# SiLU-gated split on one core: 16 rows per partition, two loads and one store of a shared output buffer

## The chip, the core and the metric

The kernel runs on one core of a Trainium2 chip. The core has five instruction streams, of which this kernel uses four: ACT (ScalarE), which applies functions elementwise, DVE (VectorE), which multiplies, SP (SyncE), which only issues transfers here, and a few constants written by POOL (GpSimd). Data move between the device's memory (HBM) and the on-chip buffers (128 partitions, each with its own stretch of memory) by DMA: an engine issues a transfer on its own queue, and 16 DMA engines, shared by all queues, carry it out. The metric is device time in microseconds (us), the median of the runs; lower is better. The profile is of one execution.

## The reference

```python
def setup_inputs():
    batch, seq, dim = (32, 512, 2048)
    return {'x': np.random.randn(batch, seq, dim).astype(np.float32)}

def reference(x: np.ndarray) -> np.ndarray:
    half_dim = x.shape[-1] // 2
    x1, x2 = (x[..., :half_dim].copy(), x[..., half_dim:].copy())
    silu_x1 = x1 * (1 / (1 + np.exp(-x1)))
    return (silu_x1 * x2).astype(np.float32)
```

There are 32 x 512 = 16,384 rows of 2,048 float32 values. SiLU of a row's first half is multiplied with its second half. The input has 134.2 MB, the output 67.1 MB, and each byte is moved once.

## The kernel before

The rows are cut into 16 tiles of 1,024 rows. In a tile, each of the 128 partitions takes K = 8 consecutive rows: 64 KiB of input in one piece of HBM, and 32 KiB of output in one piece. Neighbouring partitions of a tile lie 64 KiB apart in the input and 32 KiB apart in the output, so a tile is one closed stretch of 8 MiB in and 4 MiB out.

There are two input buffers (`in_pool`, bufs=2, L35) of 64 KiB per partition and two output buffers (`out_pool`, bufs=2, L36) of 32 KiB per partition. The function `load(i)` (L43 to L46) takes an input buffer and issues the transfer of tile i from SP (L45). Loads 0 and 1 are issued ahead of the loop; load i+2 is issued at the end of step i (L71). It goes into the buffer that tile i used, and so it waits on SP until the last multiply of tile i has read it.

A step of the loop (L50) handles one tile in four chunks of KC = 2 rows per partition. For each chunk, ACT writes SiLU of the first half into the output buffer `ot` (L56), and DVE multiplies it there with the second half (L61). After the fourth chunk ACT issues the store of the tile (L69). This instruction stands in ACT's stream behind the tile's activations and waits for the last multiply, and what follows on ACT waits with it. In the last tile each chunk is stored by itself, also from ACT (L67), 1 MiB at a time.

The order of everything else is set by buffers. The framework adds the waits: an activation waits for the load of its tile, and, where it is the first to write an output buffer again, for the landing of the store that last read that buffer. With two output buffers this is the store of two tiles earlier. Loads travel on SP's ring and stores on ACT's ring; within a ring transfers go in the order of their issue.

Of the kernel before, what the change touches and what calls it, by code (L numbers as in the profile page):

```python
# [1 line left out]

# [4 lines left out]


@with_exitstack
def kernel(  # L10
    ctx: ExitStack,
    tc: tile.TileContext,
    x: bass.AP,
    out: bass.AP,
):

    nc = tc.nc
    P = nc.NUM_PARTITIONS

    x_flat = x.flatten_outer_dims()
    out_flat = out.flatten_outer_dims()
    num_rows, in_cols = x_flat.shape
    half = in_cols // 2
    dt = x_flat.dtype

    K = 8  # L30
    KC = 2
    n_tiles = num_rows // (P * K)
    assert n_tiles * P * K == num_rows

    in_pool = ctx.enter_context(tc.tile_pool(name="in_pool", bufs=2))  # L35
    out_pool = ctx.enter_context(tc.tile_pool(name="out_pool", bufs=2))  # L36

    xv = x_flat.rearrange("(n p k) d -> n p k d", p=P, k=K)
    ov = out_flat.rearrange("(n p k) d -> n p k d", p=P, k=K)

    loaded = {}

    def load(i):  # L43
        xt = in_pool.tile([P, K, in_cols], dt, name="xt")
        nc.sync.dma_start(out=xt, in_=xv[i])  # L45
        loaded[i] = xt  # L46

    load(0)
    load(1)
    for i in range(n_tiles):  # L50
        xt = loaded.pop(i)
        last = i == n_tiles - 1
        ot = out_pool.tile([P, K, half], dt, name="ot")
        for c in range(0, K, KC):
            ce = c + KC
            nc.scalar.activation(  # L56
                out=ot[:, c:ce, :],
                in_=xt[:, c:ce, :half],
                func=mybir.ActivationFunctionType.Silu,
            )  # L60
            nc.vector.tensor_mul(  # L61
                out=ot[:, c:ce, :],
                in0=ot[:, c:ce, :],
                in1=xt[:, c:ce, half:],
            )
            if last:
                nc.scalar.dma_start(out=ov[i][:, c:ce, :], in_=ot[:, c:ce, :])  # L67
        if not last:
            nc.scalar.dma_start(out=ov[i], in_=ot)  # L69
        if i + 2 < n_tiles:  # L70
            load(i + 2)  # L71


# [1 line left out]
_INS = ['x']  # L75
_OUTS = [((32, 512, 1024), 'float32')]


# [23 lines left out]
```

## Time and profile before

| what | value |
|---|---|
| median of 3 runs | 471.87 us (471.72 to 472.5) |
| the profiled execution | 471.92 us |
| its span, first to last instruction | 470.1 us |
| DVE busy, 64 multiplies of 2,286 ns in the mean | 142.4 us, 30% |
| ACT busy, 64 activations of 1,898 ns in the mean | 118.3 us, 25% |
| bytes moved | 201.35 MB, 428 GB/s over the span |
| load, issue to landing (median of 16) | 47.1 us |
| store of a tile, issue to landing (median of 15) | 39.7 us |
| store of a chunk in the last tile (median of 4) | 5.4 us |

In the lines quoted from the profile an operation stands as line, engine, name, output <- input with partitions x elements, and count. L56 is line 56 of the kernel. In the timeline a line begins with its start and its length in us, and the bracket at its end tells how long the engine had been idle and what ended that. SPq and ACTq are the queues on which SP and ACT issue transfers; q1 is the DMA ring of SP's transfers and q10 that of ACT's. For a ring, the numbers are packets, MB moved, and the time its packets took as a share of the time of all 16 DMA engines. The row of digits after "DMA" shows the busy share of the DMA engines in 40 equal slices of the span, in tenths. In the list of waits, a line names who waited, for whom, the total in us, the number of times and the longest.

### The profile page before, as it was taken

Reading aid. Unit: us, or ns where it says so; the run is one execution under the profiler, and the core shown is the slowest. Engines: PE = TensorE matmul, PEld = TensorE weight load, DVE = VectorE, ACT = ScalarE, POOL = GpSimd, SP = SyncE. Lnnn points to the kernel's source line nnn. Section 1 sums busy time; section 2 is a strip of 40 time slices with the busy share of each in tenths; the row PEclk is TensorE's granted clock in tenths of the full one; section 3 lists DMA queues with packets and bytes.
Section 4 is the critical chain, followed back from the end, with each engine's and each line's share of the span. In section 5 each row is a group of like instructions: output and inputs, shape, how many; then the busy total and the mean of one; then the engine's idle time right before and its main releaser. Section 6 shows DMA issues by size and latency. Waiting matters only on the chain.

```text
span 470.1 us, 267 instructions
## 1 busy us (share of the span) xinstructions
DVE 142.4 (30%) x64; ACT 118.3 (25%) x65; POOL 0.2 (0%) x4
## 2 busy tenths in 40 slices
DVE  0070704207052070511606115070250702407033
ACT  1050506014060240602306032060320604106041
POOL 0000000000000000000000000000000000000000
DMA  8999999999999999999999999999999999999998
GB/s 357 446 446 401 401 485 435 418 401 443 449 446 401 441 457 396 446 474 390 468 404 438 457 441 407 427 420 449 446 410 432 480 401 418 440 474 424 399 424 337
DMA packets 5042, 201.35 MB, mean 428 GB/s; under 512 B 560, under 2 KB 560, under 8 KB 560
## 3 DMA queue, kind: packets, MB, share of 16 engines
q1 hardware_dynamic: 2304, 134.22, 66.2%
q10 hardware_dynamic: 2736, 67.11, 33.1%
q14 instruction: 2, 0.02, 0.0%
HBM read 134.22 MB, written 67.11 MB: 428 GB/s over the span
## 4 chain that ended last, share of the span: by engine, by line
DMA 80%; DVE 15%; ACT 4%; issue 0%; ACTq 0%; SPq 0%
DMA xt<-in_x_dram 80%; DVE ot L61 15%; ACT ot L56 4%; SPq L45 0%; ACTq L67 0%; ACTq L56 0%
## 5 line engine op out<-in xcount | busy, mean ns | idle before, releaser
L61 DVE TENSOR_TENSOR ot<-ot,xt 128x2048 f32<-128x2048 f32 x64 | 142.4, 2286 | 322.9 <-ACT ot L56 322.9
L56 ACT ACTIVATE ot<-xt 128x2048 f32<-128x2048 f32 x64 | 117.1, 1898 | 344.0 <-DMA xt<-in_x_dram 340.4
L56 ACT ACT_TABLE_LOAD x1 | 1.3, 1283 | 0.7 <-PEq L86 0.7
L86 POOL MEMSET const-bfloat16-1.0<- 128x1 bf16 x1 | 0.1, 101 | 0.0
L86 POOL MEMSET const-uint8-127<- 128x1 uint8 x1 | 0.1, 101 | 0.0
L86 POOL MEMSET const-float32-0.0<- 128x1 f32 x1 | 0.1, 98 | 0.2 <-issue 0.2
L86 POOL MEMSET const-float32-1.0<- 128x1 f32 x1 | 0.1, 98 | 0.0
## 6 DMA issues: line engine op xcount, KB each, us to landing
out_dram<-ot ACTq DMA_DIRECT2D x15, 4096.0 KB, 39.7
out_dram<-ot ACTq DMA_DIRECT2D x4, 1024.0 KB, 5.4
xt<-in_x_dram SPq DMA_DIRECT2D x16, 47.1
```

The costliest lines, as they stand in the source:

```text
L56: nc.scalar.activation(out=ot[:, c:ce, :], in_=xt[:, c:ce, :half], func=mybir.ActivationFunctionType.Silu,)
L61: nc.vector.tensor_mul(out=ot[:, c:ce, :], in0=ot[:, c:ce, :], in1=xt[:, c:ce, half:],)
L86: nc = _bacc.Bacc("TRN2", target_bir_lowering=False, num_devices=1)
```

## The change

A partition now takes 16 consecutive rows, in two halves of 8. Tiles are numbered as before, but tiles 2m and 2m+1 are the first and the second half of the same 128 stretches: load i brings 64 KiB per partition, with neighbouring partitions 128 KiB apart in HBM. The two tiles of a pair write into one output buffer of 64 KiB per partition, of which there is one (bufs=1), and one store of 8 MiB, 64 KiB in one piece per partition, carries the pair out; it is issued from ACT after the odd tile. The last pair differs: after tile 14 ACT stores its half of the buffer (4 MiB), and the four chunks of tile 15 are stored one by one from SP. Loads, chunks, activations and multiplies keep their sizes and numbers.

```diff
-    out_pool = ctx.enter_context(tc.tile_pool(name="out_pool", bufs=2))
+    out_pool = ctx.enter_context(tc.tile_pool(name="out_pool", bufs=1))
 
-    xv = x_flat.rearrange("(n p k) d -> n p k d", p=P, k=K)
-    ov = out_flat.rearrange("(n p k) d -> n p k d", p=P, k=K)
+    xv = x_flat.rearrange("(n p h k) d -> n h p k d", p=P, h=2, k=K)
+    ov = out_flat.rearrange("(n p k) d -> n p k d", p=P, k=2 * K)
...
-        nc.sync.dma_start(out=xt, in_=xv[i])
+        nc.sync.dma_start(out=xt, in_=xv[i // 2, i % 2])
         loaded[i] = xt
...
+    ot = None
     for i in range(n_tiles):
         xt = loaded.pop(i)
-        last = i == n_tiles - 1
-        ot = out_pool.tile([P, K, half], dt, name="ot")
+        if i % 2 == 0:
+            ot = out_pool.tile([P, 2 * K, half], dt, name="ot")
+        o0 = (i % 2) * K
         for c in range(0, K, KC):
-            ce = c + KC
+            o = slice(o0 + c, o0 + c + KC)
             nc.scalar.activation(
-                out=ot[:, c:ce, :],
-                in_=xt[:, c:ce, :half],
+                out=ot[:, o, :],
+                in_=xt[:, c:c + KC, :half],
                 func=mybir.ActivationFunctionType.Silu,
             )
             nc.vector.tensor_mul(
-                out=ot[:, c:ce, :],
-                in0=ot[:, c:ce, :],
-                in1=xt[:, c:ce, half:],
+                out=ot[:, o, :],
+                in0=ot[:, o, :],
+                in1=xt[:, c:c + KC, half:],
             )
-            if last:
-                nc.scalar.dma_start(out=ov[i][:, c:ce, :], in_=ot[:, c:ce, :])
-        if not last:
-            nc.scalar.dma_start(out=ov[i], in_=ot)
+            if i == n_tiles - 1:
+                nc.sync.dma_start(out=ov[i // 2][:, o, :], in_=ot[:, o, :])
+        if i == n_tiles - 2:
+            nc.scalar.dma_start(out=ov[i // 2][:, :K, :], in_=ot[:, :K, :])
+        elif i % 2 == 1 and i < n_tiles - 2:
+            nc.scalar.dma_start(out=ov[i // 2], in_=ot)
```

## The prediction

> **What bounds the kernel now.** I read the page's DMA parts first, then the timeline of the first tiles, the waits of SP's queue, the times from issue to landing of single DMAs, and last the end of the span.
>
> ```profile
> DMA  8999999999999999999999999999999999999998
> ...
> q1 hardware_dynamic: 2304, 134.22, 66.2%
> q10 hardware_dynamic: 2736, 67.11, 33.1%
> ```
>
> q1 is the ring of SP's loads, q10 that of ACT's stores. Together their packets fill 99.3% of 16 engines' span: nothing but data movement bounds this kernel. The packet records in the trace give the unit: a 64 KiB load packet takes 2,418 ns (median of 2,048), a 32 KiB store packet 1,213 ns (1,920), an 8 KiB store packet 309 ns (512). Per engine: 128 x 2.418 + 120 x 1.213 + 32 x 0.309 = 465.0 us of the 470.1.
>
> ```profile
> 22.75 7.31 ACT L56 ACTIVATE ot<-xt 128x2048 f32<-128x2048 f32 x4 [20.74 <-DMA xt<-in_x_dram]
> 24.69 8.90 DVE L61 TENSOR_TENSOR ot<-ot,xt 128x2048 f32<-128x2048 f32 x4 [24.69 <-ACT ot L56]
> 33.62 0.38 ACTq L69 DMA_DIRECT2D out_dram<-ot  x1
> 45.89 7.31 ACT L56 ACTIVATE ot<-xt 128x2048 f32<-128x2048 f32 x4 [15.84 <-DMA xt<-in_x_dram]
> ```
>
> A tile computes in 10.85 us: 1.95 us to the first multiply, then 8.90. It hides entirely under transfers. Note where the store is issued, 33.62, and where the next tile lands, 45.89.
>
> ```profile
> SPq L45 <- DMA xt<-in_x_dram: 246.1, 14, 21.1
> SPq L45 <- DVE ot L61: 152.5, 14, 10.9
> ```
>
> A load waits for its buffer, released by the multiplies two tiles earlier. It costs nothing now, because another load and a store are always queued. Whether that stays so is the question.
>
> ```profile
> DMA to landing us min/median/max: 33.7/33.7/33.7
> ```
>
> ```profile
> DMA to landing us min/median/max: 39.7/39.7/39.7
> ```
>
> The first is the store issued at 33.62, the second that of 114.76. In its packet records the first store's opening packet starts 5.9 us after the issue, behind the load packet in progress and one more, which here took 3.37 us, 0.95 over the usual. Then each engine alternates strictly: a store packet, a load packet, and so on; 39.55 + 8 x 1.213 + 6 x 2.418 = 63.76 (recorded: the eighth ends at 63.72). Six and not seven loads, since one turn of the load ring goes to the completion packet of a finished load. The store's own completion waits one more load packet (2.42) and 1.2 us of engine skew and signal: 67.3, the landing shown. Turns go by packet, not by byte, so a 32 KiB store gets a third of an engine. That is just its demand, and the later stores (39.7) queue behind their predecessor: both rings are never empty.
>
> **What the Trainium skill says.** "DMA: Bandwidth & Descriptors", section Queues, rings and completion order: each engine goes round its queue rows at packet granularity. The trace agrees (here a packet is one whole run of a partition). The same page, Issuing engines are not separate DMA queues: DMAs of all issuers run on the same 16 engines and interleave. The trace agrees: q1 and q10 share out one time. Its section Latency and other measured facts lists losses by row pitch in HBM: 512 KiB gives 207 GB/s where full is 214, 3% off. The new pitch of 128 KiB is not listed and no run here shows it; I keep 3% as an upper bound.
>
> **The change part by part.** *Bytes and packets.* Load packets stay at 64 KiB; their partitions now lie 128 KiB apart. Store packets become 64 KiB; by 32 to 64 KiB of load I price one at 2.418 us, so 7 pair stores, one half store and 4 last pieces give 128 x 2.418 + 56 x 2.418 + 8 x 1.213 + 32 x 0.309 = 464.5 us per engine against 465.0. Gain 0.5 us at most. ACT's, DVE's and the load issues' counts don't change; 8 store issues of 0.36 us on ACT go and 4 move to SP, all in idle time. The output buffers take the same space, one of 64 KiB for two of 32.
>
> *The added wait.* With one shared buffer, the first ACTIVATE of an even tile must wait until the whole previous pair store has landed. Behind it queue that tile's other ACTIVATEs, the odd tile's, and the next store; DVE waits for ACT; and SP's next load waits for the multiplies. So for the time store landing + 10.85 no new load can start. Only two loads are in flight to cover it.
>
> *One pair*, from C, where its store and a load B are issued. Load A, issued at the even tile's end, has run three of its 8 packet rounds and is in the fourth. First store packet at C+4.9 (current and one more load packet; 5.9 in the trace, 4.9 by the steady phase). Then 8 stores and 6 loads alternate, 14 x 2.418 = 33.85; the completion waits 2.42 + 1.2: landing at C+42.4. Load B, with a half share, has 4 of 8 rounds left and ends at C+50.9, landing C+52.1. The even tile computes from C+42.4 to C+53.25; only then is the next A issued. It starts at about 1.05 us later (the very first load: 0.73 to 1.73) and its first packet takes 0.63 longer (3.05, the mean of the first 16). The engines stand idle from C+50.9 to C+54.3. The odd tile starts with B's landing and ends at C+62.95. By then A has run three rounds again, so the cycle closes: 63.0 us a pair against 24 x 2.418 = 58.03 of work. The 5.0 lost are 3.4 idle, 0.63 and 0.95 (the stretched packet at each store's start).
>
> *Start.* Tile 0 ends at 33.6 as before. Without a store beside it load 1 ends at 41.1 and lands at 42.1 (was 45.87); tile 1 ends at C0 = 52.95. The store arrives at about 54.0 in load 2's sixth round (53.1 to 55.6), lets one more, stretched to 3.37, go by, starts at 58.9 and lands at 96.4; load 3 ends already at 100.0, but load 4 can't be issued before 107.2. Idle until 108.3. C1 = 96.4 + 1.95 + 17.8 (two tiles of multiplies back to back) = 116.15. The second pair has load 4 late and comes to C2 = 180.1; then 62.9 and 63.0 each: C6 = 432.0.
>
> *End.* Store 6 lands at 474.4, tile 14 ends at 485.25 and the half store starts at 486.3, while the loads have run out at 482.9. ACT issues it ahead of tile 15's ACTIVATEs, which so start at 485.65; the last piece is computed by 496.5. From 486.3 the half store and the pieces keep the engines busy for 8 x 1.213 + 32 x 0.309 = 19.6: 505.9, with skew 506.3. The trace has 1.26 from the last packet's end to the span's: 507.6. That the pieces come from SP costs nothing: its queue has no load left.
>
> Check by the engines: 464.5 work, 2.4 start, 1.3 end, and stalls of 9.9 (first pair), about 5 x 5.0, 0.95 for store 6 and 3.4 before the half store: 507.5. The profiled execution took 471.92 for a span of 470.1, and the median of the runs is 471.87, so 1.8 is added: **509.4 us**, 37.5 slower, 8%.
>
> **The rivals.**
>
> *Store first (not slower).* If the pair store ran nearly at full rate, it would land at about C+2+19.3+1.2 = C+22.5, and the next load, issued at C+33.4, would queue long before B ended. The point from which this decides: landing + 10.85 + 1.05 before B's end at C+50.9, a landing by C+39. Time then 464.5 + 2.4 + 1.3 = 468.2, or 470.0 us with 1.8: 0.4% faster. For it: my margin is only 3.4 us a pair. Against: the trace shows strict turns, and landing inside C+39 alone leaves the 0.95 stalls (7 x 0.95) and most of the first pair's gap, so it would still be slower. Chance 5%.
>
> *One turn later.* The store's arrival falls 0.45 us ahead of a packet boundary in my steady phase. Beyond it, each store starts 2.42 later; then the even tile ends at C+55.7 and the pair at C+65.4. Six pairs make 522 of the span, 524 us. For it: the first store in the trace came 5.9 after its issue, not 4.9. Against: the phase readjusts from pair to pair. 14%.
>
> *Smaller store packets.* If a 64 KiB run of a store were cut into two of 32 KiB, a pair store would get a third of the engine until the loads run out: 11 load rounds and 16 stores, landing near C+52; pair 52 + 19.75 = 71.5, end near 568 us. For it: no 64 KiB store packet is in the trace. Against: 64 KiB load packets are. 4%.
>
> *A wider stride costs.* 3% on 309.5 us of load packets, about 9 us more: 518. 4%.
>
> *Stalls smaller.* If the 0.95 stretch and part of the issue lag come once and not for each store, the pair takes 62 and the end is near 501. 5%.
>
> **How the numbers follow.** The likeliest case, with 68%, spans 503 to 516, its phase unknown by a part of a packet. Range 500 to 525: it takes in the later turn, the stride and the smaller stalls; outside are the first and third rivals. Slower by over 0.2% (which is what a measurement of this kernel can tell) in all but the store-first rival: 95%; of its 5%, 3 faster and 2 within, as its 0.4% gain hangs on a tail without gaps.
>
> **What would show it.** Right: ACT's waits at even tiles end with the store, not the load (some 7 of them); the store lands 42 to 44 us after issue; the DMA digits fall below 9 about every 63 us, and the mean is some 396 GB/s (428 x 470.1 / 507.6); stores and loads take 2.4 us a packet alike; C0 near 53. Wrong: store landings under 39 us, or no dip between loads, would leave the time as it was; landings above 50 would mean small packets; load packets above 2.42 us in mean, the stride.

## The result, and the profile after

The changed kernel takes 511.66 us (median of 4 runs, 510.6 to 513.12) against 471.92 us (median of 4, 471.72 to 472.5): a ratio of 1.0842, with a 95% interval of 1.0809 to 1.0875. It is slower by 8.4%. The profiled execution took 510.83 us with a span of 509.1.

First the page of the changed kernel, its row of DMA digits, its DMA parts and its list of DMA issues (the last number of an issue line is the median time from issue to landing).

```profile
DMA  9999999749999799998999989999699996999968
...
DMA packets 4035, 201.34 MB, mean 396 GB/s; under 512 B 449, under 2 KB 449, under 8 KB 449
...
q1 hardware_dynamic: 2880, 138.41, 65.3%
q10 hardware_dynamic: 1152, 62.92, 28.5%
...
xt<-in_x_dram SPq DMA_DIRECT2D x16, 37.3
out_dram<-ot ACTq DMA_DIRECT2D x7, 42.6
```

The digits dip about every 63 us, once for each pair. The packets fill 65.3 + 28.5 = 93.8% of the engines' span, where they filled 99.3%. In time: 0.938 x 509.1 = 477.5 us of packets and 31.6 of nothing, against 466.8 and 3.3. So of the 39.0 us by which the span grew, 28.3 are empty engines, and 10.7 are packets that took longer for almost the same bytes. A load lands sooner than before (37.3 us after its issue, not 47.1), and yet the kernel is slower: loads are issued later, when less is queued ahead of them.

The chain of work that ended last, by line, says what sets the end, first in the kernel before, then now:

```profile
DMA xt<-in_x_dram 80%; DVE ot L61 15%; ACT ot L56 4%; SPq L45 0%; ACTq L67 0%; ACTq L56 0%
```

```profile
DMA out_dram<-ot 59%; DVE ot L63 17%; ACT ot L58 11%; DMA xt<-in_x_dram 8%; DVEq L101 0%; SPq L45 0%; ACTq L71 0%; ACTq L58 0%
```

Before, loads were 80% of it and no store stood in it. Now stores are 59%. The lists of waits show the same change from the waiting side: ACT before, ACT now, then SP's queue now.

```profile
ACT ot L56 <- DMA xt<-in_x_dram: 340.4, 16, 21.9
```

```profile
ACT ot L58 <- DMA out_dram<-ot: 328.0, 7, 49.1
ACT ot L58 <- DMA xt<-in_x_dram: 43.8, 7, 20.5
```

```profile
SPq L45 <- DVE ot L63: 268.6, 14, 40.5
```

ACT waits seven times for a pair store, some 47 us each. The load that goes into an even tile's input buffer waits with it, since SP issues it only after that tile's multiplies: its longest wait was 10.9 us and is 40.5. The timeline shows one such pair, from one pair store to the next:

```profile
244.22 0.36 ACTq L73 DMA_DIRECT2D out_dram<-ot  x1
286.71 7.31 ACT L58 ACTIVATE ot<-xt 128x2048 f32<-128x2048 f32 x4 [46.05 <-DMA out_dram<-ot]
288.65 8.90 DVE L63 TENSOR_TENSOR ot<-ot,xt 128x2048 f32<-128x2048 f32 x4 [44.46 <-ACT ot L58]
296.32 7.31 ACT L58 ACTIVATE ot<-xt 128x2048 f32<-128x2048 f32 x4 [2.30 <-DMA xt<-in_x_dram]
298.26 8.90 DVE L63 TENSOR_TENSOR ot<-ot,xt 128x2048 f32<-128x2048 f32 x4 [0.71 <-ACT ot L58]
307.19 0.36 ACTq L73 DMA_DIRECT2D out_dram<-ot  x1
```

The store is issued at 244.22 and releases ACT at 286.71, 42.5 us later. Then come 1.94 us to the first multiply, two tiles of multiplies with 0.71 between them, and the next store: 42.5 + 1.94 + 17.8 + 0.71 = 62.95. Meanwhile the engines run dry, as a cut of the same pair into windows shows (window, length, then busy time and number of instructions of DVE, ACT and POOL, TensorE's clock, DMA share, GB/s; a packet counts in the window in which it starts, so a share can pass 1):

```profile
280.00:293.00 13.00, 4.35 (x2) 6.29 (x4) 0.00 (x0) 1.00 1.01 439
293.00:295.50 2.50, 2.50 (x3) 1.02 (x1) 0.00 (x0) 1.00 0.55 236
295.50:298.50 3.00, 2.29 (x2) 2.18 (x2) 0.00 (x0) 1.00 0.00 0
```

Both loads in flight have ended by 296, and the next is issued only when the even tile's last multiply is done, at 297.6. For some two and a half microseconds no engine moves anything.

### The profile page after: what moved, and what is told of

Same layout as the page of the kernel before. It is cut to its first block, busy times and chain, and to the rows that moved or that the text cites. A ratio compares the mean times of both kernels' runs of the same rounds, so it can differ in the third digit from the quotient of the medians.

```text
span 509.1 us, 247 instructions
## 1 busy us (share of the span) xinstructions
DVE 142.3 (28%) x64; ACT 118.1 (23%) x65; POOL 0.2 (0%) x4
## 3 DMA queue, kind: packets, MB, share of 16 engines
q1 hardware_dynamic: 2880, 138.41, 65.3%
q10 hardware_dynamic: 1152, 62.92, 28.5%
## 4 chain that ended last, share of the span: by engine, by line
DMA 67%; DVE 17%; ACT 11%; another core or an unknown queue 2%; issue 1%; DVEq 0%; ACTq 0%; SPq 0%
DMA out_dram<-ot 59%; DVE ot L63 17%; ACT ot L58 11%; DMA xt<-in_x_dram 8%; DVEq L101 0%; SPq L45 0%; ACTq L71 0%; ACTq L58 0%
## 6 DMA issues: line engine op xcount, KB each, us to landing
xt<-in_x_dram SPq DMA_DIRECT2D x16, 37.3
```

## The experiments

The theory at this point: the loss comes from the shared output buffer. The even tile waits for the landing of a store that gets half of every engine; what hangs on that landing (two tiles of multiplies, the next store, the next load) forms a closed chain longer than the transfers themselves. The rivals: the wider stride or the bigger packets cost it; the ring of the last pieces matters; or the wait would be harmless with more loads in hand. Diffs are against the kernel before or the changed kernel, as named.

### The addresses alone

Against the kernel before:

```diff
-    xv = x_flat.rearrange("(n p k) d -> n p k d", p=P, k=K)
-    ov = out_flat.rearrange("(n p k) d -> n p k d", p=P, k=K)
+    xv = x_flat.rearrange("(n p h k) d -> n h p k d", p=P, h=2, k=K)
+    ov = out_flat.rearrange("(n p h k) d -> n h p k d", p=P, h=2, k=K)
...
```

The lines left out turn the index `[i]` of each load and store into `[i // 2, i % 2]`.

> The kernel before, with the new addresses alone: partitions 128 KiB apart in the loads and 64 KiB apart in the stores, still two output buffers and one 32 KiB store per tile. Theory (the loss comes from the wait for the single shared buffer): 471.9 us, no change beyond 0.3%, load packets 2,418 ns as before. Rival (the wider stride costs): the 9 us of the upper bound of 3% or more, 480 us and up, with load packets above 2,430 ns in the median.

Measured: 471.99 us against 472.16, ratio 0.9996 (0.9988 to 1.0004). The median load packet takes 2,418 ns. Partitions 128 KiB apart in the loads, and 64 KiB apart in the stores, cost nothing that shows. The row-pitch loss that the Trainium skill lists from 512 KiB on (DMA: Bandwidth & Descriptors, Latency and other measured facts) is not there at 128 KiB.

### The last pieces from SP

The kernel before, with one word changed in L67:

```diff
-                nc.scalar.dma_start(out=ov[i][:, c:ce, :], in_=ot[:, c:ce, :])
+                nc.sync.dma_start(out=ov[i][:, c:ce, :], in_=ot[:, c:ce, :])
```

> The kernel before, with the last four pieces issued from SP instead of ACT, nothing else. Theory: no change within 0.2%, 471.9 us, since SP has nothing else to do there. Rival (ACT's activations were held back by the issue of the pieces): up to 3.5 us less, the idle time of ACT before its last activation.

Measured: 471.95 against 472.16, ratio 0.9998 (0.9990 to 1.0006): no change. The end of the kernel before, then of this run:

```profile
461.11 1.91 ACT L56 ACTIVATE ot<-xt 128x2048 f32<-128x2048 f32 x1 [3.54 <-DVE ot L61]
463.05 2.29 DVE L61 TENSOR_TENSOR ot<-ot,xt 128x2048 f32<-128x2048 f32 x1 [2.36 <-ACT ot L56]
```

```profile
452.02 7.31 ACT L56 ACTIVATE ot<-xt 128x2048 f32<-128x2048 f32 x4 [21.52 <-DMA xt<-in_x_dram]
453.97 8.90 DVE L61 TENSOR_TENSOR ot<-ot,xt 128x2048 f32<-128x2048 f32 x4 [19.93 <-ACT ot L56]
456.29 6.94 SPq L67 DMA_DIRECT2D out_dram<-ot  x4
```

ACT's stop of 3.5 us before its last activation is gone, and the last multiply ends at 462.9 instead of 465.3. It gains next to nothing, because the engines were for the most part still working off the pieces before it: by the packet records of the kernel before, a DMA engine stands idle ahead of the last piece for 0.9 us in the mean (1.4 at most). In this run none does, and the last packet ends 0.2 us earlier (468.7 for 468.9). Otherwise an engine of the kernel before is idle for 2.0 us ahead of its first packet and 1.3 behind its last, so there is little for any version to win.

### The same wait, an earlier landing: pair stores on the loads' ring

Against the changed kernel; the store is now in SP's order, behind the load in flight and ahead of the next:

```diff
-            nc.scalar.dma_start(out=ov[i // 2], in_=ot)
+            nc.sync.dma_start(out=ov[i // 2], in_=ot)
```

> The changed kernel, the seven pair stores issued from SP instead of ACT, each ahead of the load of the same step, so that it runs behind the load in flight and before the next one, at the full rate. Theory: it lands 27 to 30 us after its issue, the even tile ends about 40 us after it, before the next load runs out; no gap and no wait of the DMA engines: 470 us, at or 0.4% under the kernel before; ACT still waits for the store. Rival (layout, 64 KiB store packets or the wait by itself cost the time): 500 us or more.

Measured: 474.49 us, ratio to the kernel before 1.0044 (1.0031 to 1.0057). More than nine tenths of the loss are gone with one word. The page (digits, issues), then the waits:

```profile
DMA  8999989999999999999999999999999999999997
...
out_dram<-ot SPq DMA_DIRECT2D x7, 28.3
```

```profile
ACT ot L58 <- DMA out_dram<-ot: 224.3, 7, 33.0
```

The store lands after 28.3 us, since within a ring it need not take turns with the loads; the digits have no dips. ACT still waits seven times for it, 224.3 us in all, and that costs next to nothing: a wait is not a loss by itself. So one shared buffer is harmful only together with a landing that comes late. The expectation of 470 was 4.5 too low. The packet records give most of that: 468.0 us per engine where the bytes alone would need 464.5, with 1.07 over at the first store and 0.62 at the very first load. At 0.4% over the kernel before, this is not a version that beats both.

### The same wait, a later landing: store packets of 32 KiB

Against the changed kernel, the pair store in two halves, both written after the odd tile in the source:

```diff
-            nc.scalar.dma_start(out=ov[i // 2], in_=ot)
+            nc.scalar.dma_start(out=ov[i // 2][:, :K, :], in_=ot[:, :K, :])
+            nc.scalar.dma_start(out=ov[i // 2][:, K:, :], in_=ot[:, K:, :])
```

> The changed kernel, each pair store issued as two DMAs of half the rows, both after the odd tile, so that store packets are 32 KiB: the same bytes, the same wait, the same addresses. Theory (turns go by packet): the stores get a third of an engine while loads run, and land about 52 us after their issue; a pair takes 71.5 us, the whole about 568 us. Rival (rings share by bytes): landing near 42 and 508 to 513 us, or less, since the first half could be read out earlier.

Measured: 568.81 us, in one run. The timeline of a pair:

```profile
252.61 0.36 ACTq L73 DMA_DIRECT2D out_dram<-ot  x1
253.02 7.31 ACT L58 ACTIVATE ot<-xt 128x2048 f32<-128x2048 f32 x4 [3.97 <-DVE ot L63]
...
263.89 0.36 ACTq L74 DMA_DIRECT2D out_dram<-ot  x1
314.28 7.31 ACT L58 ACTIVATE ot<-xt 128x2048 f32<-128x2048 f32 x4 [53.95 <-DMA out_dram<-ot]
```

The run is not quite what was meant. The first half (L73) was issued at 252.61, ahead of the odd tile's activations, although the source has it behind them. So two things differ from the changed kernel: the packets, and the order of issue. The second half is issued at 263.89 and ACT goes on at 314.28, 50.4 us later instead of 42.5; and DVE stands still for 2.38 us between the two tiles instead of 0.71, because ACT waited to issue the first half. Of the 9.6 us by which a pair grows (72.55 for 62.97), 7.9 are the landing, although the first half had a start of 11.3 us, and 1.7 the stop.

The packet records show the share directly. From 253.7 to 313 us an engine carries one store packet of 32 KiB (1.21 us), one load packet of 64 KiB (2.42), one store packet, and so on: one for one, not two of the small for one of the large. Turns go by packet; the rival, sharing by bytes, is out. Both rings run empty at 313, and the engines then stand idle for some 13 us until the even tile is computed.

### An earlier landing that gained nothing: load packets of 32 KiB

Each load as two DMAs of four rows:

```diff
-        nc.sync.dma_start(out=xt, in_=xv[i // 2, i % 2])
+        H = K // 2
+        nc.sync.dma_start(out=xt[:, :H, :], in_=xv[i // 2, i % 2][:, :H, :])
+        nc.sync.dma_start(out=xt[:, H:, :], in_=xv[i // 2, i % 2][:, H:, :])
```

> The changed kernel, each load issued as two DMAs of 4 rows, so that load packets are 32 KiB and store packets stay at 64 KiB. Theory (turns go by packet, and the idle time hangs on when the store lands): the store gets two thirds of an engine and lands about 34 us after its issue instead of 42.5; the even tile is then computed before the second load ends, no gap is left, 472 to 478 us. Rival (rings share by bytes, or the loss lies in the layout or in store packets of 64 KiB): landing stays near 42, time 508 to 513 us.

Measured: 512.09 us, ratio to the kernel before 1.0824 (1.0793 to 1.0855), no better than the changed kernel. From the page and from the waits:

```profile
out_dram<-ot ACTq DMA_DIRECT2D x7, 37.4
```

```profile
ACT ot L60 <- DMA out_dram<-ot: 285.1, 7, 42.1
ACT ot L60 <- DMA xt<-in_x_dram: 93.5, 18, 11.6
```

The direction was right, the store lands after 37.4 us, but the expected gain is given back as a wait for loads: 93.5 us instead of 43.8. In the packet records (an engine's packets are found by joining each to the one that ends where it starts) one of the 16 engines falls behind. By 353 us fifteen engines have finished the load of the odd tile and stand idle, since the next load is issued only when the even tile is computed, at 354.29; one engine goes on packet by packet, and the odd tile's second half is released only at 362.73. A load counts as landed when the slowest engine is done. At the end of the loads one engine has eight load packets left when the others have none, and starts the last at 492.0, 13.9 us after the others. Why it falls behind is open; the run can't stand as support for the share of turns, and it doesn't speak against it either.

### The single buffer without the pairing

The kernel before, with one word changed in L36:

```diff
-    out_pool = ctx.enter_context(tc.tile_pool(name="out_pool", bufs=2))
+    out_pool = ctx.enter_context(tc.tile_pool(name="out_pool", bufs=1))
```

> The kernel before, with one output buffer of 32 KiB instead of two, nothing else. Theory (what costs is the wait for the store that stands between two tiles, with loads behind it): the store and one load share the engines for about 31 us, then the tile computes for 10.85 with nothing to move, 42.4 us per tile, 660 to 690 us in all. Rival (ACT's wait is hidden by the two loads in flight): 472 to 480 us.

Measured: 680.54 us, in one run. The list of waits:

```profile
ACT ot L56 <- DMA out_dram<-ot: 528.3, 15, 38.4
```

Fifteen waits for a store, 35.2 us each. The pairing of two tiles is therefore not needed for the loss; one buffer on a ring of its own is enough, and the pairing halves the number of its waits.

### One buffer or two, at half the size

At full size two shared buffers beside two input buffers would take 256 KiB of each partition, more than the 224 KiB that the Trainium skill gives (SBUF — State Buffer, Specifications (TRN2); no run here shows the limit). With `K = 4` it is half of that. First the changed kernel at half size, then the same with `bufs=2` in the output pool:

```diff
-    K = 8
+    K = 4
```

> The changed kernel with K = 4 instead of 8: the same structure at half the size, one shared output buffer. Theory: a gap at each of 16 pairs, about 34 us a pair against 29.1 of work, 535 to 550 us. Rival (the loss belongs to 64 KiB packets or to the stride of 128 KiB, both of which are gone here): below 490 us.

> The changed kernel with K = 4 and two shared output buffers, which fit at this size: it differs from the run with K = 4 and one buffer in that alone. Theory: no activation waits for a store long enough to empty the load ring, 470 to 474 us. Rival (sharing the engines evenly with a pair store costs by itself): 490 us or more.

Measured: 568.36 us with one (ratio to the kernel before 1.2047, 1.2027 to 1.2068) and 497.89 with two (1.0557, 1.0531 to 1.0582). The second buffer takes away 70 us, so the single buffer is the larger part of the loss here. But both figures are above what was expected, and that with two buffers lies in the range of the rival. For one buffer the timeline tells why:

```profile
240.68 0.36 ACTq L73 DMA_DIRECT2D out_dram<-ot  x1
265.04 7.31 ACT L58 ACTIVATE ot<-xt 128x2048 f32<-128x2048 f32 x4 [27.92 <-DMA out_dram<-ot]
266.98 8.90 DVE L63 TENSOR_TENSOR ot<-ot,xt 128x2048 f32<-128x2048 f32 x4 [26.33 <-ACT ot L58]
275.91 0.36 ACTq L73 DMA_DIRECT2D out_dram<-ot  x1
```

Here no tile waits for a load. Store, 24.4 us to ACT's release, 1.94, 8.90, store: 35.2 us a pair, a closed chain; the expectation, about 34, had the landing too early. This raised a question about my own reading, that the loads run out because too few are in flight. For two buffers, a control was needed; it comes last.

### More loads in hand

The half-size kernel with one shared output buffer and four input buffers:

```diff
-    in_pool = ctx.enter_context(tc.tile_pool(name="in_pool", bufs=2))
+    in_pool = ctx.enter_context(tc.tile_pool(name="in_pool", bufs=4))
...
     load(1)
+    load(2)
+    load(3)
...
-        if i + 2 < n_tiles:
-            load(i + 2)
+        if i + 4 < n_tiles:
+            load(i + 4)
```

> The changed kernel with K = 4, one shared output buffer, and four input buffers instead of two, four loads being issued ahead. Theory A (the time is set by the closed chain store, landing, two tiles of multiplies, next store: 24.3 + 1.95 + 8.9 = 35.2 us a pair at this size, whatever is loaded meanwhile): 555 to 570 us, no better than with two input buffers. Theory B (the loss is that no load can be issued during the wait): the loads in hand cover it, below 505 us.

Measured: 555.19 us, ratio to the kernel before 1.1755 (1.1737 to 1.1773). The waits, and then the last pair store with the activation that waits for it, first with two input buffers, then with four:

```profile
ACT ot L60 <- DMA out_dram<-ot: 405.8, 15, 28.8
ACT ot L60 <- DMA xt<-in_x_dram: 16.8, 2, 10.8
```

```profile
522.80 0.36 ACTq L73 DMA_DIRECT2D out_dram<-ot  x1
547.21 7.31 ACT L58 ACTIVATE ot<-xt 128x2048 f32<-128x2048 f32 x4 [27.97 <-DMA out_dram<-ot]
```

```profile
523.23 0.34 ACTq L75 DMA_DIRECT2D out_dram<-ot  x1
534.40 7.31 ACT L60 ACTIVATE ot<-xt 128x2048 f32<-128x2048 f32 x4 [14.74 <-DMA out_dram<-ot]
```

Twice the loads in hand save 13 us of the 96 that were lost, and none of them in the pairs: the last pair store is issued within 0.5 us of the same time in both runs. Only this last store lands earlier, after 11.2 us instead of 24.4, as the loads have run out by then. The chain through the store is as long as before (24.3 us to the landing in the median, by its page), and while it lasts the extra loads only fill their buffers sooner. What binds at half size is the chain, not the supply. At full size, where four input buffers were not tried, the two are close together: 42.5 + 1.94 + 17.8 = 62.2 us by the chain alone, 62.95 with the 0.71 us that the odd tile's load is late.

### Stores as soon as a tile is done

The changed kernel, one buffer of 64 KiB, each half stored from ACT after its own tile:

```diff
-        if i == n_tiles - 2:
-            nc.scalar.dma_start(out=ov[i // 2][:, :K, :], in_=ot[:, :K, :])
-        elif i % 2 == 1 and i < n_tiles - 2:
-            nc.scalar.dma_start(out=ov[i // 2], in_=ot)
+        if i < n_tiles - 1:
+            nc.scalar.dma_start(out=ov[i // 2][:, o0:o0 + K, :], in_=ot[:, o0:o0 + K, :])
```

> The changed kernel, with the one shared buffer of 64 KiB kept, but each half of it stored from ACT as soon as its tile is computed, in packets of 32 KiB, as the last pair's first half is. If an activation waits for the store that reads the rows it writes, the chain is opened: an even tile waits for the store of the even half only, the store ring is never empty, 472 to 476 us. If it waits for every store of the buffer, the second half's store lands some 40 us after C and the gap remains: 500 us or more.

Measured: 567.76 us, ratio 1.2012 (1.1991 to 1.2033). The timeline of a pair:

```profile
190.61 0.36 ACTq L71 DMA_DIRECT2D out_dram<-ot  x1
241.08 7.31 ACT L58 ACTIVATE ot<-xt 128x2048 f32<-128x2048 f32 x4 [54.03 <-DMA out_dram<-ot]
```

The landing of the even half's store, which was issued at 179.33:

```profile
DMA to landing us min/median/max: 32.7/32.7/32.7
```

The even half had been read out at 212.0. The next even tile, which writes just these rows, still waits until the odd half's store has landed, at 241.0: here a buffer of the pool came free as a whole. The order of issue is that of the run with store packets of 32 KiB, where the first half went out early too, and so are the times (567.76 and 568.81). Storing earlier into one buffer doesn't open the chain. Two buffers do, as the run with the addresses alone has them.

### The control at half size

The kernel before with `K = 4`.

> The kernel before with K = 4: loads in packets of 32 KiB, stores in packets of 16 KiB, two buffers of each, a store per tile. It is the control for the runs of the changed kernel at half size. Theory (what the half-size kernel with two shared buffers still loses is a load packet stretched at each start of a store into running loads, some 20 us in all, and here the store ring is never empty): 470 to 473 us. Rival (half the packet size or half the time of a load costs it): 490 us and up.

Measured: 473.81 us, ratio 1.0036 (1.0022 to 1.0049). So size is not what makes the half-size kernel with two shared buffers slow. Their pages differ in the rings; first the kernel with two shared buffers, whose span is 497.8 us, then the control, whose span is 471.6:

```profile
q1 hardware_dynamic: 4896, 136.32, 67.1%
q10 hardware_dynamic: 2304, 65.01, 30.6%
```

```profile
q1 hardware_dynamic: 4608, 134.22, 66.2%
q10 hardware_dynamic: 4752, 67.11, 33.3%
```

The first is 97.7% of 497.8, or 486 us of packets; the control's packet records sum to 468.4. Of the 26.2 us between the spans, 17.6 are longer packets and the rest are empty engines. Most of both stands at the starts of the pair stores: each time a load packet is stretched, to 1.9 to 2.5 us in the mean of the engines instead of 1.21. But in most pairs more than half of the engines had run out of load packets just there, by 0.4 us in the mean, so that the stores' ring and the loads' ring start together. Which of the two starts stretches the packet, and whether the even share costs something besides (the rival), this run doesn't separate. In the control, as in the kernel before, the store ring is hardly ever empty, and such a stretch at the start of a store happens once.

## Why the prediction was right

Forecast were 509.4 us in a range of 500 to 525; it came to 511.66. The likeliest case happened, for the most part by its own steps:

- **Bytes and packets, no gain.** Right. A 64 KiB store packet takes 2,418 ns in the median, as priced from the loads, and none is cut in two. The run with the addresses alone excludes the stride. One sign was badly chosen: "load packets above 2.42 us in mean" was to mean the stride, and the mean is 2.52 (2.43 in the kernel before), because it carries the stretched packets; the median is the one to read. The program has 7 store issues fewer, not 8, which plays no part.
- **One pair, 63.0 us.** Right: from issue to issue in a steady pair 244.22 to 307.19, 62.97. The store released ACT after 42.5 us for 42.4, but with two small errors that cancel: its first packet starts 5.4 us after the issue, not 4.9, and the rest up to the landing is shorter by nearly as much. The idle time was right (28.8 us of an engine's time between its first and last packet, where the sum by engines has 8.3 + 5 x 3.4 + 3.4 = 28.7). The stretched packets were sized a little low: 12.1 us in all for 6 x 0.63 + 7 x 0.95 = 10.4.
- **Start.** C0 was 52.7 (forecast 52.95), C1 116.64 (116.15), C2 181.07 (180.1): the load after the first gap began at 108.8, not 108.3, and the first store landed after 44.2, not 43.4. These put C6 at 433.3 instead of 432.0.
- **End.** The half store began at 487.8 (486.3) and the pieces ended at 507.7 (506.3), carried over from the start. The ring of the last pieces is without effect in the run that changes it alone.
- **Which wait binds.** Here the working was right in number and half right in cause. The step "Only two loads are in flight to cover it" makes the supply of loads the reason, and the pair's sum lets it end with the odd tile's load at C+62.95. At full size that is what comes last, by 0.71 us. But the chain store, even tile, odd tile, store needs 62.2 by itself, so more loads could have saved little; the run with four input buffers shows it at half size.
- **The rivals.** Turns by packet, on which the store-first case and that of smaller packets hang, are shown by the packet records: one for one with 64 KiB against 64 KiB, and one for one with 32 KiB against 64 KiB. On the loads' ring, where there are no turns to take, the store lands after 28.3 us and the time falls to 474.49. That the run with store packets of 32 KiB came to 568.81, where about 568 had been worked out, is in part luck: the sum has both halves issued together (and its 52 + 19.75 makes 71.75, not 71.5), while in the run the first half went out 11.3 us ahead, at the cost of a stop between the tiles. The point of decision for the store-first case, a landing by C+39, stays untested: the one run on ACT's ring that had such a landing (37.4, with 32 KiB load packets) took 512.09, but with an engine that fell behind.

The time left over is 2.3 us in the median. Of it 1.4 are in the profiled execution, about what the stretched packets have over their forecast; the other runs of the four spread by 2.5 us, where the kernel before spreads by 0.8.

## What to carry to other kernels

In a kernel bound by transfers, ask of each wait how long the ring behind it can go on without a new issue, and whether the wait closes a chain (store, landing, compute, store) that is longer than the transfers of one round; a second, smaller buffer was worth more here than a transfer of twice the size. Rings shared an engine by packets here, so the size of a packet on one ring sets the speed of the other: making a store's packets as large as the loads' gave it half the engines, and yet the chain was too long. A wait that is long in the list may cost nothing (224 us in the run with one ring, for 0.4%), and stopping an engine's idle time at the end may gain nothing: look at what the rings have queued at that moment. And read from the trace, not from the source, where an issue stands: one store here went out a tile earlier than it was written.

## What was not expected of the hardware

- A store that starts on an empty ring while loads run stretches one load packet: by 0.95 to 1.2 us in the mean of the engines, at each of the seven pair stores of the changed kernel (a packet of 3.4 to 3.6 us for 2.42). Begun on the loads' own ring, the first store still cost 1.07, the later ones 0.4 and less. The mechanism wasn't tried.
- A load ring that had run dry starts again about 1.0 us after the issue, and its first 64 KiB packet takes 3.1 to 3.2 us in the changed kernel.
- With 32 KiB load packets against 64 KiB store packets, one to three engines of sixteen were still at their loads when the others had none left, at the end of each pair's loads from 289 us on; at the very end one engine was eight packets behind. The landing waited for it. What causes it, and whether it is always the same engine, stays open.
